# Gate rows turned ahead of the seven-product stage, with two narrow gate blocks and a new block order

## The chip, the core and the metric

The kernel runs on one core of a Trainium2 chip. A core has five engines that run at the same time, each its own instructions in order: TensorE (PE, matrix products), VectorE (DVE), ScalarE (ACT), GpSimd (POOL) and SyncE (SP). They wait for each other through semaphores. DMAs are issued from the queues of SyncE and ScalarE here. The metric is the time of one execution in microseconds; the median of three runs of the kernel before is 2293.48 us (2289.91 to 2294.73).

## The reference, cut to what matters

The reference is one decoder layer in float32 with 512 tokens and a width of 2048. One wide input projection of the normalised input `u` feeds two branches; their outputs are projected back, gated, added and normalised.

```python
u = _rmsnorm(h, norm_w)
proj = jnp.matmul(u, w_in)
(ml_q, ml_k, ml_v, ml_o, ml_z, ml_i, ml_f,
 dn_qkv, dn_z, dn_b, dn_a, gate_a, gate_b) = jnp.split(proj, idx, axis=-1)

i_pre = _softcap(ml_i + ml_i_bias).transpose(0, 2, 1)
logf = jax.nn.log_sigmoid(_softcap(ml_f + ml_f_bias)).transpose(0, 2, 1)
h_a = _mlstm_chunkwise(q, k, v, i_pre, logf)           # 8 heads
h_a = _merge_heads(_rmsnorm(h_a)) * ml_norm_w
h_a = h_a * jax.nn.sigmoid(ml_o) * jax.nn.silu(ml_z)

beta = jax.nn.sigmoid(dn_b).transpose(0, 2, 1)
g = (-jnp.exp(dn_a_log) * jax.nn.softplus(dn_a + dn_dt_bias)).transpose(0, 2, 1)
h_b = _gated_delta_chunkwise(dq, dk, dv, beta, g)      # 16 heads
h_b = _merge_heads(_rmsnorm(h_b, dn_norm_w)) * jax.nn.silu(dn_z)

y = sigmoid(gate_a) * (h_a @ w_out[:2048]) + sigmoid(gate_b) * (h_b @ w_out[2048:])
out = _rmsnorm(x + y, final_norm_w)
```

The four small column groups `ml_i`, `ml_f`, `dn_b` and `dn_a` (48 columns together) are the gate rows of the title: they are summed and scanned along the tokens before either branch can use them.

## The kernel before, in words

Each float32 operand is split into a high part and a remainder (`split_hi` on ScalarE, L128; `split_lo` on VectorE, L131), and each product is made of three products of parts. Weights come by DMA on SyncE's queue into tiles `wr` (four), and their parts stand in tiles `wh` and `wl` (four each). `plan` lists all weight pieces in order of use; `next_w` loads four pieces ahead and splits three ahead.

TensorE's instructions stand in the order in which the code is written. Work of other kinds is put between its products by generators: `start(gen, wait)` enters one, and `tick()`, called once for every few products, resumes those whose waiting time has come; `yield n` waits n ticks. For the other engines a planner sets the order, by its own estimate of times and by priorities (`urgent`, `behind`, `high_priority`); on the chip each engine keeps that order.

The stages are:

1. Front. `u` is made and turned (L304 to L311), and the projection ML_Q runs with it (`proj_cm`, 96 products of 512 columns, L240 to L242, 16 ticks). The 48 gate columns are accumulated beside it in `pgr` (L318), copied to `gr0` (L342) and stored in DRAM as `gr_d` (L343). The projection ML_K follows, and one narrow block of the merge gates (`narrow_gates`, `proj_tm`, 192 products of 256 columns, L255 to L258, 16 ticks). Beside these run `u_sums` (L355 to L370), which makes eight pairs' sums of parts of `u` on GpSimd, VectorE and ScalarE, and `lead` (L550), which loads the first weight quads and prepares the first.
2. Seven-product stage (`seven`, L448). Nine blocks, each of which makes two 512-column projections from seven products of sums in place of eight: three blocks of merge gates (kind g), two of values (v), four of z and output gate (z). A block has 16 quads; a quad has three loads into `wr3`, sums on VectorE (`prep_sums`, L399: `t13` at L410, `ts` at L411 and L417), and splits (`prep_pair`). Sums of products go into the tile `X` (`U1`, `C22`) by `add` (L442). What each block does with its results is in `sink_flat` and `sink_z`, whose output tiles share the four `wr` buffers; they are stored in `tg_d`, `v_d` and `g_d`.
3. `gates` (L589 to L675) loads `gr_d` back, turns it to token columns (`pgt`, L595), computes the gate functions on VectorE and ScalarE in small tiles `sml` (L598 to L627), ten ticks later turns them to rows (`pri`, `prf`, `prg`, L636 to L638), scans the rows (L651 to L654), makes `nr`, `ar`, `er` and `iw`, stores rows in `rows_d`, and six ticks later turns rows to columns again (`pc`, L668 to L670). Two narrow gate blocks run beside this. `ml_first` prepares the first pair of mLSTM heads, from 21 ticks on.
4. Units (`UNITS`): eight pairs of DeltaNet heads (`dn_unit`, four projections each) and the other three pairs of mLSTM heads (`ml_unit`, two). A unit's recurrences run as generators under the projections of the next units; `dn_back` has short chains of TensorE and ScalarE (L880 to L915).
5. The last narrow gate block, with `load_h(0, 1)` beside it, which reloads the branch output `h` from DRAM (L1169 to L1173, ScalarE at L1171); then the output projections (L1214 and L1256 to L1258), the merge and the final norm.

The tiles of the seven-product stage (pools `sbp` and `sap`) are given up at its end, and the pool `wk` of the units takes their memory; its first writes, `gr` and `mkq` (L1128) among them, wait for that.

Of the kernel before, what the change touches and what calls it, by code (L numbers as in the profile page):

```python
# [8 lines left out]
F32 = mybir.dt.float32  # L9
# [17 lines left out]
GFIRST = (1, 3)  # L27
# [29 lines left out]
def hybrid_body(  # L57
# [31 lines left out]
    gr_d = dr.tile([112, S], F32, tag="grd", name="gr_d")  # L89
# [53 lines left out]
    add_gates(range(GFIRST[0]))  # L143
    nfront = len(plan)
    add_gates(range(*GFIRST))
# [3 lines left out]
    add_gates(range(GFIRST[1], GNARROW))  # L149
# [193 lines left out]
    nc.scalar.dma_start(gr_d, gr0)  # L343
# [27 lines left out]

    quads = [(kind, c1, c2, b, g, i) for b, (kind, c1, c2) in enumerate(SEVEN) for g in "AB" for i in range(KH)]
    rawq, partq = [], []

    def load_quad():
        if len(rawq) == len(quads):
            return
        _, c1, c2, b, g, i = quads[len(rawq)]
        with tc.high_priority(offset=2 * PRIO):
            r = sbp.tile([P, 3, NO], F32, tag="wr3", name="wr3", bufs=3)  # L380
            k1, k2 = (slice((2 * i + n) * P, (2 * i + n + 1) * P) for n in range(2))
            if g == "A":
                src = (w_in[k1, c1:c1 + NO], w_in[k1, c2:c2 + NO], w_in[k2, c2:c2 + NO])
            else:
                src = (w_in[k2, c1:c1 + NO], w_in[k2, c2:c2 + NO], t2_d[b % 2, i])
            for n in range(3):
                nc.sync.dma_start(r[:, n, :], src[n])
        rawq.append(r)

    def split(src, wide):  # L390
        if wide:
            hi, lo = (sbp.tile([P, 2, NO], F32R, tag=f"w2{n}", name=f"w{n}", bufs=2) for n in "hl")
        else:
            hi, lo = (wp.tile([P, 1, NO], F32R, tag=f"w{n}", name=f"w{n}", bufs=NSPL) for n in "hl")
        split_hi(hi, src)
        split_lo(lo, src, hi)
        return [(hi[:, n, :], lo[:, n, :]) for n in range(2 if wide else 1)]

    def prep_sums(q):  # L399

        if q >= len(quads) or q < len(partq):
            return
        _, c1, c2, b, g, i = quads[q]
        r = rawq[q]
        with tc.high_priority(offset=2 * PRIO):
            ts = wp.tile([P, 1, NO], F32, tag="tg", name="ts", bufs=3)
            if g == "A":

                t13 = sbp.tile([P, 2, NO], F32, tag="t13", name="t13")
                V.tensor_tensor(out=t13, in0=r[:, 1:3, :], in1=r[:, 0:2, :], op=ALU.subtract)  # L410
                V.tensor_tensor(out=ts[:, 0, :], in0=r[:, 2, :], in1=t13[:, 0, :], op=ALU.subtract)  # L411
                p_ = split(ts, False)
                nc.scalar.dma_start(t2_d[b % 2, i], ts[:, 0, :])
                partq.append((p_ + split(r[:, 0:1, :], False), t13))
            else:

                V.tensor_tensor(out=ts[:, 0, :], in0=r[:, 0, :], in1=r[:, 2, :], op=ALU.subtract)  # L417
                partq.append((split(ts, False), r[:, 0:2, :]))

    def prep_pair(q):  # L420
        if q < len(quads):
            p_, pair = partq[q]
            with tc.high_priority(offset=2 * PRIO):
                w2 = split(pair, True)
            partq[q] = p_ + w2 if quads[q][4] == "A" else w2 + p_

    JW, OO = ((psj, "pj"), (psw, "wk")), ((pso, "o"),) * 2

    def half2(t):
        return slice(HP + t.start, HP + t.stop)  # L430

    LHS = {"A": (lambda i, t: (suh[:, i, 1, t], sul[:, i, 1, t]),
                 lambda i, t: (uh[:, 2 * i, t], ul[:, 2 * i, t]),
                 lambda i, t: (suh[:, i, 0, t], sul[:, i, 0, t]),
                 lambda i, t: (suh[:, i, 2, t], sul[:, i, 2, t])),
           "B": (lambda i, t: (uh[:, 2 * i + 1, t], ul[:, 2 * i + 1, t]),
                 lambda i, t: (s4h[:, i, t], s4l[:, i, t]),
                 lambda i, t: (uh[:, 2 * i + 1, half2(t)], ul[:, 2 * i + 1, half2(t)]))}

    def add(x, a, b):  # L440
        with urgent(3):
            V.tensor_tensor(out=x, in0=a, in1=b, op=ALU.add)  # L442

    def copy1(t, p1):
        with urgent(3):
            A.copy(U1[t], p1)

    def seven(n0, kind, c1, c2):  # L448

        m6, m1, m5, m7 = ([pool.tile([P, NO], F32, tag=t, name="ps") for pool, t in banks_] for banks_ in (OO, JW, JW, JW))  # L450
        ends = {"A": (None, lambda t: (copy1(t, m1[t]), add(U1[t], U1[t], m6[t])),
                      lambda t: add(C22[t], U1[t], m5[t]), lambda t: add(C22[t], C22[t], m7[t])),
                "B": SINK[kind](c1, c2, m1, m5, m7)}
        for n in range(2 * KH):
            g, i = "AB"[n // KH], n % KH
            prep_sums(n0 + n + 1)
            prep_pair(n0 + n + 1)
            load_quad()
            if n == 2 * KH - 2:

                prep_sums(n0 + n + 2)
            if n0 + n == len(quads) - 1:
                limit[0] = len(plan)
                prepare(nfront - 1)
            for m, ps in enumerate((m6, m1, m5, m7) if g == "A" else (m1, m5, m7)):
                hi, lo = partq[n0 + n][m]
                for t in range(2):
                    ah, al = LHS[g][m](i, slice(t * P, (t + 1) * P))
                    T.matmul(ps[t], ah, hi, start=(g == "A" and i == 0), stop=False, skip_group_check=True)  # L469
                    T.matmul(ps[t], ah, lo, start=False, stop=False, skip_group_check=True)  # L470
                    T.matmul(ps[t], al, hi, start=False, stop=(i == KH - 1), skip_group_check=True)  # L471
                    if i == KH - 1 and ends[g][m] is not None:
                        ends[g][m](t)
                tick()

    def stored(q, d, x_):
        with behind("A"):
            nc.scalar.dma_start(d, x_)
        yield 1

    def sink_flat(dst, func, scale):

        def sink(c1, c2, m1, m5, m7):
            def out_(ps, c, col):
                o = wp.tile([P, NO], F32, tag="wr", name="to", bufs=NRAW)
                with urgent(3):
                    A.activation(o, ps, func, scale=scale)  # L487
                nc.scalar.dma_start(dst(c, col), o)

            def late(x_, c, col):  # L490
                with behind("A"):
                    if func != AF.Copy:
                        A.activation(x_, x_, func, scale=scale)
                    nc.scalar.dma_start(dst(c, col), x_)
                yield 1

            def end5(t):
                add(m5[t], U1[t], m5[t])
                out_(m5[t], t, c2)
                start(late(C22[t], 2 + t, c2), 1)  # L500

            def end7(t):
                add(U1[t], U1[t], m7[t])
                start(late(U1[t], 2 + t, c1), 2)

            return (lambda t: out_(m1[t], t, c1)), end5, end7
        return sink

    def sink_z(c1, c2, m1, m5, m7):

        col = c1 - ML_Z
        zs = {}

        def end1(t):
            z = wp.tile([P, NO], F32, tag="wr", name="to", bufs=NRAW)
            with urgent(3):
# [4 lines left out]
        def end5(t):  # L521
            add(m5[t], U1[t], m5[t])
            with urgent(3):
# [4 lines left out]
        def late(t):  # L528
            th = wp.tile([P, NO], F32, tag="wr", name="to", bufs=NRAW)
            with behind("A"):  # L530
                A.activation(th, U1[t], AF.Tanh, scale=0.5)
                A.activation(C22[t], C22[t], AF.Tanh, scale=0.5)
# [790 lines left out]
```

## Time and profile before

| what | value |
|---|---|
| median of three runs | 2293.48 us |
| the profiled execution | 2289.74 us |
| its span, first to last instruction | 2288.0 us |
| mean granted TensorE clock | 0.993 |
| TensorE busy | 2219.1 us (97%) |
| VectorE busy | 1516.8 us (66%) |
| ScalarE busy | 892.2 us (39%) |
| GpSimd busy | 262.0 us (11%) |
| DMA traffic | 384.97 MB, mean 168 GB/s |

In the rows of the profile `L240` is line 240 of the kernel, PE to SP are the engines (`SPq` and `ACTq` their DMA queues), `out<-in` are the program's tiles, and `xN` counts instructions. A row of the timeline gives start and duration in us, and in brackets the idle time of the engine before the instruction and what ended it. A row of the waits gives who waited for whom, the total in us, how often and the longest. A row of the windows gives length, the busy time of each engine with its count of instructions, the granted clock, the share of the DMA engines and GB/s.

### The profile page before, as it was taken

The numbers are of one execution on the slowest core, as the hardware profiler recorded it, in microseconds if no ns is written. First come the engines' busy times: TensorE is split into PE (matmuls) and PEld (weight loads), VectorE is DVE, ScalarE is ACT, GpSimd is POOL, SyncE is SP. The second block draws the span as 40 slices with busy tenths as digits, with TensorE's granted clock in tenths as the row PEclk, the third lists the DMA queues.
The fourth block names the chain that finished last, engine by engine and source line by source line (L and its number), as shares of the span: only waits on it lengthen the run. The fifth ranks groups of instructions, "written<-read, shape, count | busy, mean of one in ns | idle before, by whom it ended". The sixth has DMA issues, their size and how long they took to land.

```text
span 2288.0 us, 33006 instructions
## 1 busy us (share of the span) xinstructions
PE 2219.1 (97%) x11599; PEld 1857.0 (81%) x11599; DVE 1516.8 (66%) x2721; ACT 892.2 (39%) x1768; POOL 262.0 (11%) x329
## 2 busy tenths in 40 slices
PE   6999999999999989999999999999999999999998
PEld 5878887878777878878887888888888889987886
DVE  5878777777887854858367673868458685434445
ACT  4344444444444433433343343343343344222223
POOL 0700000000000001202022110212013210000111
PEclk9999999999999989999999999999999999999999
DMA  5367767776666646557466484656566465865333
GB/s 152 115 200 229 232 182 226 228 221 184 207 210 186 216 135 165 138 128 189 109 157 145 118 208 105 163 135 170 137 146 152 118 161 181 247 209 162 116 116 131
DMA packets 503721, 384.97 MB, mean 168 GB/s; under 512 B 238369, under 2 KB 402434, under 8 KB 503554
## 3 DMA queue, kind: packets, MB, share of 16 engines
q1 hardware_dynamic: 406146, 333.26, 51.9%
q10 hardware_dynamic: 97408, 49.60, 7.4%
q8 instruction: 91, 1.49, 0.3%
q14 instruction: 76, 0.62, 0.1%
HBM read 310.09 MB, written 72.65 MB: 167 GB/s over the span
## 4 chain that ended last, share of the span: by engine, by line
PE 69%; DMA 12%; DVE 10%; issue 3%; ACT 2%; SPq 2%; POOL 1%; ACTq 0%; DVEq 0%; POOLq 0%
PE pj L240 12%; PE pj L241 11%; PE pj L242 11%; PE ps L469 5%; PE ps L470 5%; PE ps L471 5%; DVE wl L131 4%; DMA wr<-t_d 3%; PE py L1257 3%; PE py L1258 3%; PE py L1256 3%; DMA wr<-in_w_in_dram 2%; DMA hr<-h_d 2%; PE pjt L255 1%; PE pjt L258 1%
## 5 line engine op out<-in xcount | busy, mean ns | idle before, releaser
L131 DVE TENSOR_TENSOR wl<-wr,wh 128x512 fp32r<-128x512 f32 (+1 forms) x624 | 490.1, 789 | 354.4 <-ACT wh L128 333.5
L128 ACT CAST wh<-wr 128x512 fp32r<-128x512 f32 (+1 forms) x624 | 415.9, 669 | 722.0 <-PE pj L241 359.3
L240 PE MATMUL pj<-uh,wh 128*128 128x512 f32 x1280 | 530.1, 414 | 3.8 <-ACT thz L721 3.2
L242 PE MATMUL pj<-uh,wl 128*128 128x512 f32 x1280 | 501.3, 392 | 0.0
L241 PE MATMUL pj<-ul,wh 128*128 128x512 f32 x1280 | 500.5, 391 | 0.6 <-DVE ul L310 0.6
L242 PEld LDWEIGHTS pj<-uh,wl 128*128 128x128 f32 x1280 | 240.6, 188 | 52.8
L240 PEld LDWEIGHTS pj<-uh,wh 128*128 128x128 f32 x1280 | 241.6, 189 | 50.4 <-ACT thz L721 3.6
L241 PEld LDWEIGHTS pj<-ul,wh 128*128 128x128 f32 x1280 | 241.8, 189 | 43.9 <-DVE ul L310 0.9
L469 PE MATMUL ps<-wh,suh 128*128 128x512 f32 x432 | 169.6, 393 | 6.1 <-DVE X L442 2.5
L470 PE MATMUL ps<-wl,uh 128*128 128x512 f32 x432 | 169.4, 392 | 1.7 <-DVE wl L131 1.7
L469 PE MATMUL ps<-wh,uh 128*128 128x512 f32 x432 | 169.2, 392 | 1.6 <-DVE X L442 0.9
L470 PE MATMUL ps<-wl,suh 128*128 128x512 f32 x432 | 168.3, 390 | 0.7 <-DVE wl L131 0.7
L471 PE MATMUL ps<-wh,ul 128*128 128x512 f32 x432 | 168.2, 389 | 0.0
L471 PE MATMUL ps<-wh,sul 128*128 128x512 f32 x432 | 168.2, 389 | 0.0
L257 PE MATMUL pjt<-wl,uh 128*128 128x256 f32 x512 | 147.6, 288 | 2.8 <-DVE wl L131 2.8
L255 PE MATMUL pjt<-wh,uh 128*128 128x256 f32 x512 | 149.8, 293 | 0.0
L128 ACT CAST wh<-ts 128x512 fp32r<-128x512 f32 x144 | 89.0, 618 | 151.0 <-DVE ts L417 126.2
L258 PE MATMUL pjt<-wh,ul 128*128 128x256 f32 x512 | 147.3, 288 | 0.0
L128 ACT CAST wh<-t 128x1024 fp32r<-128x1024 f32 x72 | 75.8, 1053 | 181.8 <-DVE ts L411 80.4
L131 DVE TENSOR_TENSOR wl<-t,wh 128x1024 fp32r<-128x1024 f32 x72 | 89.1, 1238 | 47.8 <-ACT wh L128 47.7
L131 DVE TENSOR_TENSOR wl<-ts,wh 128x512 fp32r<-128x512 f32 x144 | 98.6, 690 | 20.8 <-ACT wh L128 20.8
L469 PEld LDWEIGHTS ps<-wh,suh 128*128 128x128 f32 x432 | 81.1, 188 | 28.0 <-ACT to L487 4.5
(284 smaller groups left out, 3705.7 us busy)
## 6 DMA issues: line engine op xcount, KB each, us to landing
wr<-in_w_in_dram SPq DMA_DIRECT2D x712, 256.0 KB, 3.5
wr<-in_w_out_dram SPq DMA_DIRECT2D x128, 256.0 KB, 3.2
t_d<-ts ACTq DMA_DIRECT2D x72, 256.0 KB, 3.6
wr<-t_d SPq DMA_DIRECT2D x72, 256.0 KB, 4.1
tgl<-tg_d SPq DMA_DIRECT2D x24, 256.0 KB, 3.5
xt<-in_x_dram SPq DMA_DIRECT2D x8, 512.0 KB, 7.9
v<-v_d SPq DMA_DIRECT2D x8, 512.0 KB, 5.6
mg<-g_d SPq DMA_DIRECT2D x16, 256.0 KB, 3.3
```

Source lines behind the costliest of these rows:

```text
L128: newest["A"] = A.copy(hi, src).ins
L131: newest["V"] = V.tensor_tensor(out=lo, in0=src, in1=hi.bitcast(F32), op=ALU.subtract).ins
L240: T.matmul(ps[j], hi[:, k, wsl], uh[:, kt, :], start=(kt == 0), stop=False)
L241: T.matmul(ps[j], hi[:, k, wsl], ul[:, kt, :], start=False, stop=False)
L242: T.matmul(ps[j], lo[:, k, wsl], uh[:, kt, :], start=False, stop=(kt == KT - 1))
L255: T.matmul(o, uh[:, kt, tsl], hi[:, k, :], start=(kt == 0 and c % 2 == 0), stop=False, skip_group_check=True)
L257: T.matmul(o, uh[:, kt, tsl], lo[:, k, :], start=False, stop=False, skip_group_check=True)
L258: T.matmul(o, ul[:, kt, tsl], hi[:, k, :], start=False, stop=(kt == KT - 1), skip_group_check=True)
L469: T.matmul(ps[t], ah, hi, start=(g == "A" and i == 0), stop=False, skip_group_check=True)
L470: T.matmul(ps[t], ah, lo, start=False, stop=False, skip_group_check=True)
L471: T.matmul(ps[t], al, hi, start=False, stop=(i == KH - 1), skip_group_check=True)
L1256: T.matmul(ps[c], hh[base][:, kt, tsl], hi[:, 0, :], start=(kt == 0), stop=False)
```

## The change

`gates` moves from behind the seven-product stage to its front: it starts with ML_K, takes `gr0` from its tile, without the store to and load from DRAM, and keeps its rows in the stage's own tiles (`wr3` for rows, `t13` for `sml`) before the first quads need them. Some rows reuse others' places, so `ar` is made before `nr`, and `er` after `iw`. `u_sums` starts 8 ticks later and `lead` at 38 ticks in place of 24. Two narrow gate blocks stand ahead of the stage in place of one, none at the head of the units in place of two, and two behind the units in place of one, with `load_h` beside the second. `ml_first` starts one tick into the first unit.

In the stage the order of the blocks is z, g, v. The sums of a block's first quad are made one quad sooner. `sink_z` only copies the first product out of PSUM and takes one tanh of the second ahead of the next block; the rest follows later. The last block's output tiles come from `tg` in place of `wr`.

```diff
-GFIRST = (1, 3)
+GFIRST = 2
...
-SEVEN = ([("g", GATE + c, GATE + c + NO) for c in range(GNARROW * NB, 2 * D, 2 * NO)]
-         + [("v", ML_V + c, ML_V + c + NO) for c in range(0, 2 * D // 2, 2 * NO)]
-         + [("z", ML_Z + c, ML_O + c) for c in range(0, D, NO)])
+SEVEN = ([("z", ML_Z + c, ML_O + c) for c in range(0, D, NO)]
+         + [("g", GATE + c, GATE + c + NO) for c in range(GNARROW * NB, 2 * D, 2 * NO)]
+         + [("v", ML_V + c, ML_V + c + NO) for c in range(0, D, 2 * NO)])
...
-    nc.scalar.dma_start(gr_d, gr0)
...
     def gates():
-        gr0 = wk.tile([112, S], F32, tag="th", name="gr1", bufs=3)
-        nc.sync.dma_start(gr0, gr_d)
-        yield 5
+        rows = [sbp.tile([P, 3, S], F32, tag="wr3", name="grow", bufs=3) for _ in range(3)]
+
+        def row(n, i):
+            return rows[i // 3][0:n, i % 3, :]
+
...
-        sml = wk.tile([P, 10, NC, 24], F32, tag="ls", name="sml", bufs=1)
+        sml = sbp.tile([P, 2, NO], F32, tag="t13", name="sml").rearrange("p a n -> p (a n)")[:, 0:240 * NC]
...
+        iw, ar, nr, er = row(MLH, 7), ir, br, mr
+        V.tensor_tensor(out=ar, in0=ir, in1=br, op=ALU.subtract)
         V.tensor_tensor(out=nr, in0=br, in1=mr, op=ALU.subtract)
-        V.tensor_tensor(out=ar, in0=ir, in1=br, op=ALU.subtract)
-        A.activation(er, mr, AF.Exp, scale=-1.0)
...
+        A.activation(er, mr, AF.Exp, scale=-1.0)
...
     def seven(n0, kind, c1, c2):
...
-            if n == 2 * KH - 2:
+            if n == 2 * KH - 3:
 
-                prep_sums(n0 + n + 2)
+                prep_sums(n0 + n + 3)
...
+    def spare(last):
+        return wp.tile([P, NO], F32, tag="tg" if last else "wr", name="to", bufs=3 if last else NRAW)
...
     def sink_z(c1, c2, m1, m5, m7, last):
...
         def end1(t):
-            z = wp.tile([P, NO], F32, tag="wr", name="to", bufs=NRAW)
+            zs[t] = spare(False)
             with urgent(3):
-                A.activation(z, m1[t], AF.Tanh, scale=0.5)
-                V.scalar_tensor_tensor(out=z, in0=z, scalar=1.0, in1=m1[t], op0=ALU.add, op1=ALU.mult)
-            zs[t] = z
+                A.copy(zs[t], m1[t])
 
         def end5(t):
             add(m5[t], U1[t], m5[t])
+            os_[t] = spare(False)
             with urgent(3):
-                A.activation(m5[t], m5[t], AF.Tanh, scale=0.5)
-                V.scalar_tensor_tensor(out=zs[t], in0=m5[t], scalar=1.0, in1=zs[t], op0=ALU.add, op1=ALU.mult)
-            start(stored(None, g_d[t, :, col:col + NO], zs[t]), 1)
+                A.activation(os_[t], m5[t], AF.Tanh, scale=0.5)
+            start(late(zs[t], os_[t], t), 2 + 2 * t)
...
-    start(u_sums())
-    start(lead(), 24)
+    start(gates())
+    start(u_sums(), 8)
+    start(lead(), 38)
     spill(proj_cm(ML_K), 2, 1.0)
-    for b in range(GFIRST[0]):
+    for b in range(GFIRST):
         narrow_gates(b)
...
-    start(gates())
-    start(ml_first(*ml_new(0)), 21)
-    for b in range(*GFIRST):
-        narrow_gates(b)
+    start(ml_first(*ml_new(0)), 1)
     for kind, p in UNITS:
         (dn_unit if kind == "d" else ml_unit)(p)
...
-    start(load_h(0, 1), 4)
-    for b in range(GFIRST[1], GNARROW):
+    for b in range(GFIRST, GNARROW):
+        if b == GNARROW - 1:
+            start(load_h(0, 1), 4)
         narrow_gates(b)
```

More of the change, by code (lines that the diff above doesn't have):

```diff
@@ L370, in u_sums @@
             yield 3
[L372 to L458, printed above, removed]
-            if n == 2 * KH - 2:
-                prep_sums(n0 + n + 2)
[L462 to L507, printed above, removed]
@@ L638, in gates @@
             T.transpose(prg[0:DNH, tsl], sp[:, c, 8:24], ident)
[L640 to L643 removed]
+        ir, fr, gr, msk = row(MLH, 0), row(MLH, 1), row(DNH, 2), row(DNH, 3)
         A.copy(ir, pri[0:MLH, :])
```

225 lines of the change are left out of this document (164 added, 61 removed).

## The prediction

> **What bounds the kernel now.** I read the page first, then the windows by stage, TensorE's waits, and the timelines of the three places that the change touches. From the page:
>
> ```profile
> PE 2219.1 (97%) x11599; PEld 1857.0 (81%) x11599; DVE 1516.8 (66%) x2721; ACT 892.2 (39%) x1768; POOL 262.0 (11%) x329
> PEclk9999999999999989999999999999999999999999
> PE 69%; DMA 12%; DVE 10%; issue 3%; ACT 2%; SPq 2%; POOL 1%; ACTq 0%; DVEq 0%; POOLq 0%
> ```
>
> TensorE is busy 97% of the span, and the change removes none of its products. So only stretches in which TensorE waits, or runs at a lower granted clock, can move the time. These windows enclose the places (us, PE busy, PEld, DVE, ACT, POOL, granted clock, DMA share, GB/s):
>
> ```profile
> 58.60:80.30 21.70, 21.70 (x97) 17.77 (x96) 17.59 (x15) 10.41 (x18) 16.93 (x14) 1.00 0.69 217
> 80.30:108.30 28.00, 25.23 (x194) 24.73 (x193) 23.61 (x21) 9.62 (x17) 21.47 (x19) 0.94 0.20 58
> 108.30:119.00 10.70, 7.29 (x31) 5.11 (x30) 9.21 (x10) 3.57 (x8) 6.63 (x5) 1.00 0.46 148
> 818.00:837.00 19.00, 8.48 (x71) 8.31 (x71) 7.70 (x13) 4.14 (x8) 2.74 (x14) 0.79 0.67 207
> 837.00:843.00 6.00, 6.00 (x30) 6.00 (x31) 3.83 (x15) 0.80 (x3) 0.00 (x0) 0.51 0.63 216
> 843.00:877.00 34.00, 34.00 (x291) 33.59 (x290) 18.29 (x40) 10.28 (x20) 1.65 (x4) 1.00 0.55 159
> 1893.00:1909.00 16.00, 13.32 (x150) 12.58 (x150) 8.04 (x13) 9.65 (x17) 0.00 (x0) 0.89 0.60 185
> ```
>
> The first row, the second projection (ML_K), has no wait: 96 products in 21.7 us, 0.226 us each. A product of a narrow gate block is half as wide; 843:877 gives 34.0 / 291 = 0.117 with two dozen transposes among them, and I use 0.12, so 192 of them are 23.0 us. TensorE's waits, by who ended them:
>
> ```profile
> PE pgt L595 <- DMA mkq<-qk_d: 10.5, 1, 10.5
> PE ps L469 <- DVE X L442: 4.8, 12, 0.9
> PE pjt L257 <- DVE wl L131: 2.8, 2, 2.2
> PE ps L470 <- DVE wl L131: 2.4, 3, 1.5
> PE p L895 <- ACT s L889: 1.5, 2, 1.3
> PE p L906 <- DVE ta L902: 1.2, 1, 1.2
> ```
>
> **The change, part by part.** The sum is made against the profiled execution, 2289.74 us, of which 2288.0 is the span; the median of the runs, 2293.48, stands 3.7 above it, and I add that at the end.
>
> (a) The 10.5 us wait goes. It lies between the seven-product stage and the units: the gate rows came back from DRAM only after SyncE's queue had issued seven weight loads, and those began late, since the last blocks (kind z) held their tiles until stored.
>
> ```profile
> 823.51 7.80 SPq L165 DMA_DIRECT2D wr<-in_w_in_dram  x7
> 831.48 0.34 SPq L591 DMA_DIRECT2D gr<-gr_d  x1
> 831.87 1.84 SPq L1128 DMA_DIRECT2D mkq<-qk_d  x4
> ```
>
> With it goes a stretch at half clock: in 837:843, at 0.51, 30 products and transposes went in 6.0 us where 6.0 / 0.12 = 50 would have gone, 20 x 0.12 = 2.4 us. Together -12.9. What is late next there: the changed program's order on SyncE has the four mkq loads, which wait for the stage's memory, behind weight loads for eight sub-steps of the first unit, 8 x 12 x 0.226 = 21.7 us of cover; the first product that reads mkq stands 13 ticks of six products in, 13 x 1.36 = 17.7 us, while before the loads began some 14 us after the stage. The first unit now shares VectorE and ScalarE with head pair 0, which had two narrow blocks to itself; I take +1, between 0 and the 5 us that a lost row broadcast would cost (12 us late less the cover above).
>
> (b) The narrow block in front and the start of the stage. 80.30:108.30 took 28.0 for 23.0 us of products: 5.0 lost. 108.30:119 ran 31 products, 31 x 0.226 = 7.0 of 10.7 us: 3.7 lost. Both are VectorE arrears (wl L131 above): it makes the sums of u, weight splits and the first quad's sums together, busy 23.61 of 28 us. After the change a second narrow block, 23 us, stands there, u_sums starts 8 ticks later and lead at 38 of 48 ticks, so the arrears are worked off before the stage. Of 8.7 I take 7.2 back (bounds 0 and 8.7).
>
> (c) The tail. In 1893:1909 PE is busy 13.32 of 16 us, 2.7 idle, at clock 0.89, (1 - 0.89) x 16 = 1.7: 4.4 lost. ScalarE stood at the reloads of h (L1171) while the last unit's L889 and L900 waited behind it:
>
> ```profile
> 1895.53 0.72 ACT L1171 ACTIVATE uh<-hr,normc 128x512 fp32r<-128x512 f32 x1 [1.03 <-DMA hr<-hm_d]
> 1896.78 0.78 ACT L889 ACTIVATE s<-p 32x256 f32<-32x256 f32 x2
> ```
>
> Now a narrow block of 16 ticks is between, and load_h begins in the second one: -4.4 (bounds -4.4 and 0).
>
> (d) Block edges. The ps waits on X at L442 are 4.8 us over 12 times. Earlier first sums, and z sinks that take only a copy or one tanh ahead of the next block, may take 2 of that; two more ScalarE copies per z block, 8 x 0.6 us, are hidden (ACT 39%). -2, bounds -4.8 and +3.
>
> (e) The new cost: the row transposes. All of the gate arithmetic, one block in the old trace, moves into ML_K, among u_sums and the splits. VectorE runs in order, and TensorE reaches the transposes of pri, prf, prg after 11 ticks. Rows of the old trace for what stands ahead of them, and for the chain itself:
>
> ```profile
> 58.63 0.40 PE L240 MATMUL pj<-uh,wh 128*128 128x512 f32 x1
> 60.27 0.73 POOL L362 TENSOR_TENSOR X<-X 128x256 f32<-128x256 f32 x1 [42.33 <-DVE X L359]
> 72.47 1.21 DVE L359 TENSOR_TENSOR X<-uh,ul 128x1024 f32<-128x1024 f32 x1
> 74.47 0.41 DVE L369 TENSOR_TENSOR s4l<-X,s4h 128x256 fp32r<-128x256 f32 x1
> 78.68 3.21 POOL L359 TENSOR_TENSOR X<-uh,ul 128x1024 f32<-128x1024 f32 x1
> 78.68 0.96 DVE L369 TENSOR_TENSOR sul<-X,suh 128x768 fp32r<-128x768 f32 x1 [1.50 <-ACT suh L368]
> 79.56 2.62 DVE L369 TENSOR_TENSOR s4l<-X,s4h 128x256 fp32r<-128x256 f32 x1
> 82.73 1.18 POOL L364 TENSOR_TENSOR X<-X 128x256 f32<-128x256 f32 x1
> 837.92 0.36 DVE L598 COPY gt<-pgt 128x192 f32<-128x192 f32 x1 [7.00 <-DMA mkq<-qk_d]
> 843.70 0.69 DVE L131 TENSOR_TENSOR wl<-wr,wh 128x512 fp32r<-128x512 f32 x1 [1.25 <-ACT wh L128]
> 848.54 0.26 DVE L622 TENSOR_TENSOR sml<-sml 128x96 f32<-128x96 f32 x1
> 850.19 0.22 DVE L627 SCALAR_TENSOR_TENSOR sml<-sml 128x64 f32<-128x64 f32 x1
> ```
>
> ML_K begins at 58.63, so TensorE is there at 58.63 + 66 x 0.226 + four transposes (0.8) = 74.4. In the changed program's order on VectorE the last links of the gate chain stand behind the sul and s4l of the third K pair. GpSimd paces those; nothing of the change makes it faster, and in the old trace that s4l ended at 82.18. Behind it come L620, L621, L622, L623, L624 and L627, about 1.5 us by their starts: 83.7 at the earliest. The chain alone is 8 us (12.5 from its first row to its last, less three splits like the one shown, 0.6 each, and 2.4 of waits), on top of the 17.59 busy us of 58.6:80.3, less some later splits, so I take 84.8. The wait is 10.4 us, as long as the one removed, and I give it the same half-clock price: +12.8 (bounds 9.3 without a clock loss, and 19).
>
> (f) The second row wait. After 12 transposes, 30 products and half a gate sub-step TensorE wants pc. By then VectorE must copy two rows, scan three, make ar and nr with two sul, an X and two splits between; ScalarE then has ML_K's two spills, a split, four exps and er.
>
> ```profile
> 857.01 1.20 DVE L653 TENSOR_TENSOR_SCAN br<-msk,fr 8x512 f32<-8x512 f32 x1
> 861.88 0.97 ACT L661 ACTIVATE iw<-nr,mr 8x128 f32<-8x128 f32 x3
> 859.36 0.63 ACT L658 ACTIVATE er<-mr 8x512 f32<-8x512 f32 x1 [3.14 <-DVE mr L654]
> ```
>
> VectorE: 3 x 1.13 for the scans, 4 x 0.62 for copies and differences, 0.9 + 1.2 + 0.4 for the u ops, 2 x 0.62 to 1.2 for splits: some 10 to 11 us from the rows' arrival; then iw and er, 0.3 + 0.97 + 0.63. That is 12 to 13 us against 1.0 (copies overlap transposes) + 30 x 0.226 + 1.5 = 8.3 to 9. Wait 4, and 1.7 for half clock: +5.7 (bounds 1 and 9). If ScalarE's late spills were all, it would be 1.
>
> By the rule of the Trainium skill, page TensorE: Matmul & The Clock Gate, section Part 1: The HAM clock gate, an idle window of about 3.4 us halves the clock until a busy window has passed; the clock part of (e) would then be 1.7 to 3.4, an estimate from that page, where I took 2.4 from 837:843; the 0.51 of that row agrees with a half.
>
> Removed DMAs (one store, one load of gate rows) and moved transposes cost nothing net. Sum: -12.9 + 1 - 7.2 - 4.4 - 2 + 12.8 + 5.7 = -7.0. Profiled 2282.7, median 2286.4; I say 2286.
>
> **The rivals.**
> R1, the row transposes are covered: the chain's order lets TensorE through with under 5 us in (e) and (f). For it: 18.5 us of front wait is more than any place of the old trace shows. Against: s4l of pair three ended at 82.18. Time 2286 - 13 = 2273.
>
> R2, slower: VectorE and GpSimd take turns on the gate chain. s4l takes 0.41 us alone and 2.62 beside GpSimd's add, ending when that does (82.18 against 81.89). If each of the chain's 12 two-input ops waits out half of a 0.73 to 1.2 us GpSimd op, 12 x 0.5 = 6 more at (e), 3 at (f), and the arrears reach the stage, so that (b) gives nothing, 7: 2286 + 16 = 2302. It decides from 7 us of extra lateness on. Against: ops of 0.2 us fit between GpSimd's. The Trainium skill, page SBUF — State Buffer, section Who interferes with whom, has it that a VectorE instruction with two SBUF inputs blocks fully while a GpSimd instruction that reads SBUF holds their shared port; the s4l row agrees, and R2 is what that rule would make of the chain.
>
> R3, no change: the wait is only moved, 12.9 gone in the middle and 18.5 come in front, with (b), (c) and (d) giving about 6: 2293. That the middle wait stays, as a wait of the first unit on mkq, is the form in which the change would not do what it says; the 17.7 us of cover speak against it.
>
> **How the numbers follow.** Within 0.2% (4.6 us) a measurement cannot tell a change here. Forecast 0.45, of which 0.35 ends below 2288.9 and 0.10 within; its own range is 2279 to 2293. R1 0.20, faster. R2 0.20, slower. R3 0.15: 0.12 within, 0.03 faster. Faster 0.58, same 0.22, slower 0.20. The range runs from below R1, with (d) at its better bound, 2269, to R2, 2302.
>
> **What would show it.** Right: no wait over 2 us between the last ps product and the first unit, granted clock 1.00 there; a wait of 8 to 13 us at the prf transposes ended by VectorE, one of 2 to 6 at pc ended by ScalarE's er, both followed by a 0.5 clock; the narrow blocks after them and the first quads without wl waits; L889 and L900 of the last unit without waits. Wrong: front waits under 5 us in all (R1), narrow blocks and quads still waiting for wl (R2), or new waits over 5 us in the first two units.

## The result, and the profile after

The changed kernel takes 2298.76 us, the kernel before 2291.4 us (medians of 13 runs each): a ratio of 1.0037, with an interval of 1.0027 to 1.0047. It is slower by 0.4%, some 8 us, where 2286 was predicted. The profiled execution took 2297.73 us. From its page:

```profile
PE 2220.8 (97%) x11599; PEld 1856.4 (81%) x11599; DVE 1514.0 (66%) x2721; ACT 896.3 (39%) x1776; POOL 262.0 (11%) x329
PEclk9799999999999999999999999999999999999999
```

Busy times stand as before. The dip of the clock in the second slice is new. The windows of the stages tell where the time went; first the kernel before: ML_K up to the seven-product stage (the front), that stage, the middle, the units, the tail up to the first output projection, and the rest (columns as in the prediction):

```profile
58.60:108.40 49.80, 47.03 (x290) 42.61 (x288) 41.30 (x35) 20.13 (x35) 38.50 (x32) 0.97 0.41 127
108.40:817.40 709.00, 697.36 (x3026) 563.86 (x3025) 552.98 (x690) 311.65 (x444) 6.53 (x5) 1.00 0.66 205
817.40:879.70 62.30, 51.78 (x414) 51.16 (x413) 31.12 (x70) 17.71 (x37) 4.58 (x19) 0.89 0.61 178
879.70:1878.90 999.20, 990.76 (x5390) 824.33 (x5389) 680.63 (x1603) 388.97 (x978) 182.16 (x236) 1.00 0.60 146
1878.90:2011.00 132.10, 129.06 (x1143) 127.85 (x1142) 60.10 (x97) 44.55 (x91) 5.89 (x8) 0.99 0.69 207
2011.00:2288.00 277.00, 263.05 (x1154) 215.56 (x1152) 120.69 (x175) 80.41 (x144) 21.03 (x16) 0.99 0.45 145
```

The same of the changed kernel, where the middle is only 0.2 us:

```profile
59.00:153.30 94.30, 76.08 (x509) 70.50 (x508) 69.71 (x91) 31.85 (x59) 43.57 (x38) 0.87 0.35 102
153.30:864.00 710.70, 698.99 (x3026) 563.59 (x3025) 546.82 (x691) 314.90 (x449) 0.00 (x0) 1.00 0.65 203
864.20:1866.90 1002.70, 992.31 (x5388) 825.19 (x5387) 681.73 (x1607) 390.34 (x982) 188.57 (x253) 1.00 0.61 151
1866.90:2021.60 154.70, 150.92 (x1334) 149.43 (x1333) 66.65 (x108) 52.14 (x105) 5.53 (x8) 1.00 0.66 198
2021.60:2295.90 274.30, 262.28 (x1154) 215.89 (x1152) 118.94 (x172) 78.47 (x140) 21.03 (x16) 0.99 0.44 143
```

A narrow block is 23.0 us. Two left the middle, one went to the front and one to the tail. Less these, the front grew by 94.3 - 49.8 - 23.0 = 21.5 us, the middle fell by 62.3 - 46.0 - 0.2 = 16.1, the tail by 0.4 and the rest by 2.7; the stage grew by 1.7 and the units by 3.5. With 0.4 us by which ML_K begins later that is +7.9, the difference of the spans. So the middle gave what it was to give; the front took more, and the stage, the units and the tail gave nothing. Among TensorE's waits in the changed kernel (left out is the longest, 15.1 us for a load at the start, which was 15.0 before):

```profile
PE prf L426 <- DVE sml L413: 12.6, 1, 12.6
PE pcs L1053 <- DVE kw L1042: 6.8, 5, 3.9
PE pc L455 <- ACT grow L446: 5.6, 1, 5.6
PE ps L559 <- DVE X L532: 4.5, 10, 1.6
PE ps L560 <- DVE wl L130: 3.5, 6, 0.8
PE pr L931 <- DVE st L952: 1.5, 1, 1.5
PE pst L946 <- ACT w L942: 1.4, 1, 1.4
```

The waits at pgt, at L889's and at L902's results (the kernel before's lines) are gone. In their place stand the two row waits of the front, one at pcs in the first unit and two in the last DeltaNet chain. Behind the first three of them the clock is a half (windows of the changed kernel):

```profile
87.40:91.50 4.10, 4.10 (x16) 2.91 (x17) 1.84 (x4) 1.61 (x3) 0.00 (x0) 0.50 0.00 0
104.80:112.00 7.20, 7.20 (x38) 7.17 (x39) 5.08 (x9) 1.87 (x4) 4.92 (x7) 0.50 0.65 172
901.20:907.30 6.10, 6.10 (x14) 4.83 (x15) 2.94 (x5) 4.46 (x14) 2.58 (x4) 0.50 0.84 200
```

At half speed, half of each stretch is lost: 2.1, 3.6 and 3.1 us. The first wait ends with the gate chain on VectorE. Rows of that chain, of a split among it and of GpSimd beside it, from the timeline of the changed kernel:

```profile
61.77 0.42 DVE L394 TENSOR_TENSOR sml<-grow,bia 128x64 f32<-128x64 f32 x1
63.70 2.72 POOL L356 TENSOR_TENSOR X<-uh,ul 128x1024 f32<-128x1024 f32 x1
64.09 2.37 DVE L398 TENSOR_SCALAR sml<-sml 128x32 f32<-128x32 f32 x1
79.06 2.34 POOL L356 TENSOR_TENSOR X<-uh,ul 128x1024 f32<-128x1024 f32 x1
79.08 2.43 DVE L409 TENSOR_TENSOR sml<-sml 128x96 f32<-128x96 f32 x1
83.43 0.42 DVE L366 TENSOR_TENSOR s4l<-X,s4h 128x256 fp32r<-128x256 f32 x1
87.19 0.22 DVE L416 SCALAR_TENSOR_TENSOR sml<-sml 128x64 f32<-128x64 f32 x1
```

L394 to L416 takes 25.6 us. The two steps shown, of 32 and of 96 elements, start just after a wide add of GpSimd and end when it ends (66.46 and 66.42 us, 81.51 and 81.40): VectorE and GpSimd take turns.

### The profile page after: what moved, and what is told of

Read it like the earlier page. It is cut to its first block, busy times and chain, and to the rows that moved or that the text cites. A ratio compares the mean times of both kernels' runs of the same rounds, so it can differ in the third digit from the quotient of the medians.

```text
span 2295.9 us, 32990 instructions
## 1 busy us (share of the span) xinstructions
PE 2220.8 (97%) x11599; PEld 1856.4 (81%) x11599; DVE 1514.0 (66%) x2721; ACT 896.3 (39%) x1776; POOL 262.0 (11%) x329
## 4 chain that ended last, share of the span: by engine, by line
PE 73%; DVE 10%; DMA 9%; issue 3%; ACT 2%; SPq 2%; POOL 0%; ACTq 0%; DVEq 0%; POOLq 0%
PE pj L238 11%; PE pj L239 11%; PE pj L240 11%; PE ps L560 6%; PE ps L559 6%; PE ps L561 5%; DVE wl L130 4%; PE py L1249 3%; PE py L1250 3%; PE py L1248 3%; DMA wr<-in_w_in_dram 2%; PE pjt L253 2%; PE pjt L255 2%; PE pjt L256 2%; DMA wr<-t_d 2%
## 5 line engine op out<-in xcount | busy, mean ns | idle before, releaser
L500 DVE TENSOR_TENSOR t<-wr 128x1024 f32<-128x1024 f32 x72 | 87.8, 1219 | 20.9 <-DMA wr<-in_w_in_dram 20.5
```

## The experiments

T1: the loss is made in front, because the gate chain shares VectorE with the sums of u and takes turns with GpSimd, and its results come later than the products between can cover. The rivals: VectorE's arrears have a fixed size and only surface there; or the loss lies in the stage (sums, z sinks) or at the first unit. Names and lines in the diffs are those of the changed kernel; all ratios are to the kernel before, with the changed kernel at 1.0037.

**More products between.**

```diff
-        yield 10
+        yield 20
...
-        yield 6
+        yield 10
```

> T1 (the gate chain reaches TensorE late because it shares VectorE with the sums of u and their splits, and the changed kernel gives it too few products of cover: 11 ticks before the transposes of prf, some 30 products before pc): with 10 more ticks of ten half-width products and 4 more before pc, the waits at prf (12.6 us) and pc (5.6) and the half clock behind them (2.2 and 3.7) go, to under 4 us in all, and nothing else moves: 18 to 20 us faster than the changed kernel, about 2279, so also faster than the kernel before by some 12. Rival A (the arrears of VectorE only show there and are paid further on): the prf and pc waits go, but waits of ps or of the gate product for wl of 8 to 15 us in all come in the second narrow block and the first quads, and the time falls by 5 us or less. Rival B (the products in between need work of VectorE that stands behind the chain): the waits stay above 10 us.

2292.68 us, 1.0007 (0.9994 to 1.0019): some 6 us faster, a third of what T1 gave. The wait at prf is gone, the front 84.3 us in place of 94.3. But pc still waits 4.4 us, and at 86.2 the first narrow block waits 3.9 us for its bank, which ML_K's spill (L333) has to empty. ScalarE:

```profile
88.79 0.83 ACT L365 CAST suh<-X 128x768 fp32r<-128x768 f32 x1 [5.88 <-POOL X L360]
89.53 0.59 ACT L333 ACTIVATE qk<-pj 128x512 f32<-128x512 f32 x1
```

The spill stands behind a split of the sums of u, which waits 5.9 us for GpSimd. The gate chain is no shorter; its last step begins 28.7 us after ML_K does, 28.2 in the changed kernel. So cover alone isn't enough: it hides the chain without making it shorter, and the spill's wait takes its place.

**The sums of u behind the gate chain.** The first wide add waits for the chain's last VectorE step.

```diff
-            E.tensor_tensor(out=uf, in0=uh[:, 2 * i:2 * i + 2, :].bitcast(F32), in1=ul[:, 2 * i:2 * i + 2, :].bitcast(F32),
-                            op=ALU.add)
+            with ExitStack() as after_:
+                if i == 0:
+                    after_.enter_context(behind("gate"))
+                E.tensor_tensor(out=uf, in0=uh[:, 2 * i:2 * i + 2, :].bitcast(F32),
+                                in1=ul[:, 2 * i:2 * i + 2, :].bitcast(F32), op=ALU.add)
...
-        V.scalar_tensor_tensor(out=sp[:, :, 8:24], in0=sp[:, :, 8:24], scalar=-1.0,
-                               in1=ea.unsqueeze(1).to_broadcast([P, NC, 16]), op0=ALU.mult, op1=ALU.mult)
+        newest["gate"] = V.scalar_tensor_tensor(out=sp[:, :, 8:24], in0=sp[:, :, 8:24], scalar=-1.0,
+                               in1=ea.unsqueeze(1).to_broadcast([P, NC, 16]), op0=ALU.mult, op1=ALU.mult).ins
```

> The first add of the sums of u is held until the last VectorE step of the gate chain has been issued, so the chain runs without those sums and without GpSimd beside it. T1: the wait at prf falls from 12.6 to between 0 and 4 us, that at pc from 5.6 to between 2 and 6 (the sums of u then stand between the scans); the stage's first quads start with sums that end some 12 us later, cover 20 us, so few of them wait: 10 to 14 us faster than the changed kernel, about 2287. Rival A (arrears are only moved): prf falls, and the same 10 to 13 us come back as wl or sul waits at the start of the seven-product stage. Rival C (the chain is slow by its own length and the splits of ML_K): prf stays above 9 us.

2287.40 us, 0.9986 (0.9975 to 0.9997): 11 us faster than the changed kernel, as T1 had it. No wait at prf is left. The chain's seven repeats of two steps, first in the changed kernel:

```profile
L409 DVE TENSOR_TENSOR sml<-sml x7: 249/258/2432, 71.8 to 83.8; 128x96 f32<-128x96 f32 x7
L410 DVE TENSOR_SCALAR sml<-sml x7: 195/210/723, 72.1 to 84.6; 128x96 f32<-128x96 f32 x7
```

and here (shortest, median and longest in ns, first and last start in us):

```profile
L412 DVE TENSOR_TENSOR sml<-sml x7: 251/259/259, 68.8 to 73.7; 128x96 f32<-128x96 f32 x7
L413 DVE TENSOR_SCALAR sml<-sml x7: 201/209/211, 69.1 to 74.0; 128x96 f32<-128x96 f32 x7
```

All of the chain's VectorE steps on `sml` sum to 7.1 us here and to 16.9 in the changed kernel: 9.8 us of the chain are turns with GpSimd. From its first row to its last it takes 11.5 us in place of 25.6; the other 4.3 us are the sums and splits that no longer stand between. The wait at pc is 6.7 us in two pieces, just above the 2 to 6 expected, with a half clock behind it.

**No wide add on GpSimd.**

```diff
-            E = V if i % 2 == 0 else G
+            E = V
```

> All four wide adds of the sums of u go on VectorE (1.2 us each) and none on GpSimd (3 us each). If turns with GpSimd stretch the gate chain (rival R2 of the prediction, in its mechanism): the two-input steps of the chain that took 0.7 to 2.4 us beside GpSimd go to 0.3 us, the wait at prf falls by 3 to 6 us and the time by 4 to 8. If VectorE's own load sets it: VectorE has 2.4 us more to do ahead of the transposes, and the wait at prf is 0 to 3 us longer, the time the same or up to 4 us longer.

2291.79 us, 0.9997 (0.9986 to 1.0009): 7 us faster, the wait at prf 9.9 us in place of 12.6 and the one at pc 3.4 in place of 5.6. VectorE has four adds more in the front and yet is busy 63.9 us there, not 69.7. So its load isn't the bound; the turns are. The rest of the chain is still stretched by GpSimd's 256-element steps (L409's median here is 0.67 us).

**er ahead of iw.**

```diff
-        iw, ar, nr, er = row(MLH, 7), ir, br, mr
+        iw, ar, nr, er = row(MLH, 7), ir, br, fr
...
+        A.activation(er, mr, AF.Exp, scale=-1.0)
         A.activation(iw[:, 0:P], nr[:, 0:P], AF.Exp)
...
-        A.activation(er, mr, AF.Exp, scale=-1.0)
```

> The row er is computed ahead of the three exps of iw instead of behind them, in a row of its own. If the wait at pc (5.6 us, ended by ScalarE's er) is set by ScalarE's order: it falls by 1.0 to 1.5 us and the time by 1 to 2 us, within what can be told. If it is set by the scans on VectorE alone, er starts no earlier and the wait is 5 to 6 us. No theory expects more than 2.5 us here; the wait at prf stays at 12 to 13.

2295.22 us, 1.0017 (1.0006 to 1.0027), 3.5 us faster: more than any theory allowed. The wait at pc is gone; 1.6 us for the spill stand in its place. ScalarE in the changed kernel, then here:

```profile
100.09 0.83 ACT L365 CAST suh<-X 128x768 fp32r<-128x768 f32 x1 [4.84 <-POOL X L360]
104.10 0.63 ACT L446 ACTIVATE grow<-grow 8x512 f32<-8x512 f32 x1
```

```profile
95.63 0.63 ACT L443 ACTIVATE grow<-grow 8x512 f32<-8x512 f32 x1 [2.68 <-DVE grow L438]
100.50 0.83 ACT L365 CAST suh<-X 128x768 fp32r<-128x768 f32 x1 [3.73 <-POOL X L360]
```

er is made from the row mr alone, whose scan (L439) ended at 92.1 in the changed kernel. But there er is written over mr, so it has to stand behind nr and the exps of iw, which still read mr, and with them behind a split of the sums of u that waited 4.84 us for GpSimd. The edit writes er over fr instead; it starts when the last scan that reads fr (L438) has ended, 8.5 us sooner.

**The first sums of a block one quad later, as before the change.**

```diff
-            if n == 2 * KH - 3:
+            if n == 2 * KH - 2:
...
-                prep_sums(n0 + n + 3)
+                prep_sums(n0 + n + 2)
```

> The changed kernel with the first sums of a block's first quad made when they were before. If making them one quad sooner is what puts VectorE behind at the block's second half (the waits on X at the ninth quad, up to 1.75 us, in 5 of 9 blocks): these shrink and the stage falls from 710.7 to 707 or 708 us. If making them sooner helps at the edges, as the prediction had it: waits at the first quad come back, 0.7 to 1.3 us a block, and the stage takes 713 to 718. If neither: 709 to 712, and no difference in time beyond 2 us.

2296.59 us, 1.0033 (1.0021 to 1.0044); by time alone it can't be told from the changed kernel. The stage can:

```profile
154.70:861.70 707.00, 696.85 (x3026) 563.94 (x3025) 548.72 (x691) 315.60 (x449) 0.00 (x0) 1.00 0.66 205
```

707.0 in place of 710.7, and this holds in every kernel here: the seven with the changed z handling and early sums take 709.7 to 712.0 us, the five with late sums 705.8 to 708.5. So the early sums cost 3 to 4 us. The waits on X stay, though (4.8 us in 9, in place of 4.5 in 10), those at the ninth quad among them (up to 1.2 us): that they are the way by which it costs is not shown.

**The old handling of the z blocks.** `sink_z` and `late` as they were: both tanh and their products ahead of the next block, the first store at once.

```diff
-                A.copy(zs[t], m1[t])
+                A.activation(z, m1[t], AF.Tanh, scale=0.5)
+                V.scalar_tensor_tensor(out=z, in0=z, scalar=1.0, in1=m1[t], op0=ALU.add, op1=ALU.mult)
...
-            start(late(zs[t], os_[t], t), 2 + 2 * t)
+            start(stored(None, g_d[t, :, col:col + NO], zs[t]), 1)
```

> The changed kernel with the old handling of the z blocks' results (both tanh and the products taken ahead of the next block). The prediction put a gain of some 2 us on the new handling. If it gives one: the waits of 0.8 to 1.0 us at the third quad (four blocks) move back to the first, and the stage is 1 to 4 us longer, 712 to 715. If the new handling only moves the wait: the stage stays at 709 to 712 and the time within 2 us of the changed kernel. If it costs: the stage falls by 2 or more. The front stays as it is, at 89 to 94 us.

2300.93 us, 1.0049 (1.0033 to 1.0066), the stage 713.6 us, and the waits on X 9.6 us in 15 in place of 4.5 in 10. By time it can't be told from the changed kernel either; the stage is 1.6 us above the longest of the seven. As expected, the waits at the third quad of the four blocks behind a z block move back to the first, and grow from 0.4 to 0.8 us to 1.2 to 1.3. So the new handling gives some 3 us, as the prediction had it; the early sums take them back.

**One narrow block back at the head of the units, one behind them.**

```diff
-GFIRST = 2
+GFIRST, GHEAD = 2, 1
...
     start(ml_first(*ml_new(0)), 1)
+    for b in range(GFIRST, GFIRST + GHEAD):
+        narrow_gates(b)
```

> The changed kernel with one narrow block back between the stage and the units, so head pair 0 has 23 us of products without another unit beside it; one narrow block is left behind the units, with the reload of h in it, as before the change. If head pair 0 in the first unit costs what the units lost (3.9 us at pcs and half a clock from 900.5 to 907.3, 3.4): both go, and the way from the stage's end to the last projection is 5 to 7 us shorter. If two narrow blocks behind the units are what took away L889's and L900's waits at the last unit: those come back, 4.4 us, and the sum is 0 to 3 us faster. If neither: within 2 us of the changed kernel. The front stays.

2300.48 us, 1.0047 (1.0029 to 1.0065): no gain. Units, tail, and the two waits in question:

```profile
887.40:1885.40 998.00, 990.29 (x5380) 824.27 (x5380) 683.04 (x1603) 390.71 (x980) 184.62 (x239) 1.00 0.60 148
1885.40:2018.60 133.20, 130.34 (x1142) 129.01 (x1141) 59.85 (x97) 44.53 (x91) 5.90 (x8) 0.97 0.69 206
```

```profile
PE pcs L1054 <- DVE kw L1043: 5.8, 3, 4.5
PE p L890 <- ACT s L884: 2.0, 1, 2.0
```

The wait at pcs stays at 4.5 us: a narrow block for head pair 0 ahead of the first unit doesn't take it away. Less that block, the way from the stage's end to the tail is 3.7 us shorter (1002.9 to 999.2), but the tail is 1.5 and the rest 3.8 longer. With one block behind the units ScalarE's wait comes back (2.0 us) with a half clock of 6.8 us: the tail is 133.2 - 23.0 = 110.2 us in place of 108.7. The mechanism of step (c) is there; in the tail it is worth 1.5 us.

**pc later, behind the sums edit.** As the second experiment, and

```diff
-        yield 6
+        yield 12
```

> As the kernel whose sums of u wait for the gate chain (2287.4 us, span 2285.8), and pc six ticks later. There the waits at pc were 2.1 and 4.6 us, 6.7 in all, and half a clock followed from 90.6 to 97.4, 3.4 us lost. T1 (only cover is lacking, the row work itself is short): six more ticks are 8.6 us of products, so pc does not wait, nor does the clock fall there: 9 to 10 us less, about 2278, the front from ML_K to the stage 73 to 75 us in place of 83.5. Rival A (the arrears are moved on): the pc wait goes, but the narrow blocks wait for ScalarE's tgs (2.2 us already) and the first quads for sul or wl, 5 us or more in all: about 2283 or above.

2285.71 us, 0.9977 (0.9965 to 0.9989), the front 78.7 us. pc no longer waits, but 5.9 us of other waits come instead, as the rival had it: the narrow blocks wait 3.1 and 0.9 us, the second quad 1.9. VectorE:

```profile
108.34 1.76 DVE L503 TENSOR_TENSOR t<-wr 128x1024 f32<-128x1024 f32 x1 [1.30 <-DMA wr<-in_w_in_dram]
110.03 1.22 DVE L130 TENSOR_TENSOR wl<-wr,wh 128x512 fp32r<-128x512 f32 x1
```

The rows stand in the tiles of the first quads until pc is done, so these loads come late, and the narrow block's weight split is queued behind the sum that waits for them.

**All that helped, and two more edits.** The ninth kernel has the second experiment's edit, er first, late sums, and `yield 8`. The tenth adds to it the first line below, the eleventh the second, the twelfth both.

```diff
-    start(ml_first(*ml_new(0)), 1)
+    start(ml_first(*ml_new(0)), 5)
...
-            E = V if i % 2 == 0 else G
+            E = V
```

> The sums of u wait for the gate chain; er is computed ahead of the exps of iw; pc comes 2 ticks later (8, where 12 put the return of the rows' tiles, and so the first quads' loads, too late: 1.3 us of VectorE waiting for a load with the weight splits behind it); the first quad's sums are made when they were before the change. T1: no wait at prf, none or under 1 us at pc, no wl wait over 1 us in the narrow blocks, one half clock of 3.4 us at most in the front: front 73 to 77 us (78.7 with pc at 12 ticks, 94.3 in the changed kernel), stage 707 to 709, about 2279 to 2281. Rival (VectorE's arrears in front have a fixed size, 8 us or so, whatever the order): the front stays at 78 to 81 us and the time at 2283 to 2286.

> The same with the first mLSTM head pair started 4 ticks later in the first unit. If the wait at pcs (4 to 5 us, with half a clock for 3.4 to 6.8 us behind it) comes from the pair's rows and keys, that arrive over DRAM at a fixed time after the stage: 4 ticks are 5.4 us of products, the wait goes, and the units take 997 to 999 us in place of 1001 to 1003: 3 to 5 us faster than the same kernel without it. If the wait is VectorE's work of the first unit and the pair's own, in turn: it moves by 4 ticks and stays, within 1.5 us.

> As the first of these, with all four wide adds of the sums of u on VectorE, none on GpSimd. With the chain out of the way the adds stand beside splits only. If GpSimd's long adds hold VectorE up still (s4l 2.6 us beside them, 0.4 alone): the sums end earlier, ScalarE's tgs no longer waits behind suh, the front is 2 to 4 us shorter. If VectorE is the bound there: 0 to 2 us longer.

> The two last edits together: head pair 0 four ticks later, and no long add of the sums of u on GpSimd. If they are independent (one works at the first unit, one in the front): front 75 us, units 995, so some 4 us below the kernel with the later head pair alone, 2274 to 2275, a ratio to the kernel before of 0.992 to 0.993. If both only gave the same arrears another place: no better than the better of the two, 2278.

| kernel | median, us | ratio (interval) | front, us | stage | units |
|---|---|---|---|---|---|
| ninth | 2281.09 | 0.9952 (0.9933 to 0.9970) | 79.7 | 708.4 | 1002.6 |
| tenth | 2278.22 | 0.9939 (0.9923 to 0.9955) | 78.7 | 708.5 | 995.4 |
| eleventh | 2279.75 | 0.9947 (0.9929 to 0.9965) | 75.1 | 707.6 | 1001.0 |
| twelfth | 2277.09 | 0.9946 (0.9928 to 0.9964) | 75.1 | 705.8 | 998.7 |

All four beat both kernels; among themselves they can't be told apart by time. In the ninth the time came as said, but the front did not: 79.7, inside the rival's range, with 4.5 us of wl waits and 2.0 for tgs. The eleventh shows what about half of these arrears are. Front of the ninth and of the eleventh:

```profile
60.60:140.40 79.80, 73.26 (x510) 68.04 (x510) 66.57 (x91) 31.64 (x59) 48.66 (x38) 0.98 0.39 111
```

```profile
58.90:134.00 75.10, 72.87 (x509) 67.92 (x508) 62.93 (x95) 31.34 (x59) 35.60 (x34) 0.98 0.41 118
```

With four adds more VectorE is busy 3.6 us less and TensorE done 4.6 us sooner (3.6 us in the twelfth against the tenth): the arrears have no fixed size. The ninth's front is 8.8 us longer than its products (21.7, 46.0 and 3.2 us); some 4 of these are turns with GpSimd. ScalarE's tgs, against what was expected, still holds TensorE up for 1.9 us. In the tenth the first wait at pcs falls from 4.0 to 0.8 us, and no half clock follows:

```profile
890.43 0.67 PE L1056 MATMUL pcs<-v,kw 128*128 128x257 f32 x2 [0.79 <-DVE kw L1045]
```

In the changed kernel and in the seventh, kw was scaled 36 and 38 us after the stage's end, without a narrow block between and with one. What it stood behind in the changed kernel:

```profile
899.40 0.69 DVE L130 TENSOR_TENSOR wl<-wr,wh 128x512 fp32r<-128x512 f32 x1 [0.91 <-ACT wh L127]
900.01 1.12 DVE L1042 TENSOR_TENSOR kw<-kw,we 128x512 f32<-128x512 f32 x1
```

kw goes to DRAM and back, but its load, issued at 887.36, had landed by 894.2 (no transfer of kw took over 6.8 us). VectorE came to it some 6 us later, behind a split of a weight of the first unit (`wl`). The first half of that split, `wh` on ScalarE, began at 898.75, after 2.47 us of waiting for the weight's load. The seventh, ninth and eleventh kernels have the same order; in the tenth and the twelfth the split ahead waits for no load. So what comes last is a weight load, not kw; why these loads are late, no run here takes apart. Whether the last two edits add up stays open: the twelfth's profiled execution is the shortest (span 2268.1 us), but its median can't be told from those of the tenth and the eleventh.

## Why the prediction was wrong

The sign was wrong. No single step explains it: the terms came out worse by 15 us together (+7.9 for -7.0). The two waits in front stood where the prediction put them, and every sign that it named for being right came; so did one of those for being wrong, new waits of over 5 us in the first two units (5.3 at pcs). The bounds held but for (d) and (f), by 1.0 and 0.2 us; the values chosen between them did not.

| step | predicted | measured | how |
|---|---|---|---|
| (a) the middle | -12.9 | -12.9 | -16.1, of which 3.2 is 27 transposes that moved in front, 0.117 us each as in 843:877 |
| (a) first unit | +1 | +3.5 | units 999.2 to 1002.7 |
| (b) narrow block in front | -5.0 | -5.6 | what is left of the front's +21.5 less 3.2, 14.7 and 9.2 |
| (b) start of the stage | -2.2 | -2.3 | its first block, 81.6 to 79.3 us |
| (c) tail | -4.4 | -0.4 | tail 132.1 to 154.7, less 23.0 |
| (d) block edges | -2 | +4.0 | stage +1.7, less the first block |
| (e) wait at prf | +12.8 | +14.7 | 12.6 and 2.1 of clock |
| (f) wait at pc | +5.7 | +9.2 | 5.6 and 3.6 of clock |
| ML_K's start | 0 | +0.4 | |
| output projections and after | 0 | -2.7 | 277.0 to 274.3 us |

(d) failed most, by 6 us, and in sign. "Earlier first sums ... may take 2 of that": they cost 3 to 4 (fifth experiment). What the z sinks gave (3 us, sixth) is lost on them. Some 3 to 4 us more lie in the three blocks of kind g, which take 236.2 us before, the arrears at the stage's start included, 237.0 in the changed kernel and 237.3 in the fifth experiment; the four z blocks take 315.5, 315.4 and 312.9, the two v blocks 157.7, 158.8 and 157.2. Why isn't known: the block order wasn't tried by itself. The first block is of kind g before and z after, so the line between (b) and (d) is a rough one: by the waits in it before, 3.4 us, (b) would be -3.4 there and (d) +5.1.

(c) failed by 4 us. L889 and L900 no longer hold TensorE up, as forecast, which is the 2.7 us of waits and 1.7 of clock. But the step took what is gained there as gained in all, and the last DeltaNet chain waits behind them instead: 3.8 us at pr, pst and po, where 0.4 were before. The 2.7 us at the end are no term of the prediction: the output projections wait 0.7 us for their weights' splits in place of 2.5. The fourth kernel, whose code is the same from there on, waits 4.1 and takes 279.3 us for that part, so this gain isn't firm.

(f) was mis-sized by 3.5 us, 1.6 of wait and 1.9 of clock (7.2 us at half, where 3.4 were reckoned). VectorE's part came as reckoned, 10.9 us from the rows' arrival to the end of nr. ScalarE then needed 4.1 us to the end of er, not 1.9: the prediction listed the work ahead of er but priced it by busy time, and one split among it had waited for GpSimd, with two spills and two more splits behind it (fourth experiment). "If ScalarE's late spills were all, it would be 1" looked at the right queue; what held it was the split ahead of them. The terms on TensorE's side also add up to 9.3 us, not to 8.3 to 9.

(e) was mis-sized by 1.9 us. The last links do stand behind s4l of the third pair, which ended at 83.9 (82.2 in the old trace). But the chain was priced by rows of the old trace beside which GpSimd stood nearly still, where by the same trace it is busy 16.9 of 21.7 us in the new place: the links left, to the end of L416, took 3.6 us, not 1.5. R2 named the mechanism, and its 6 us were too few for the chain itself, 9.8 (second experiment); only 2.2 of them were new at the wait, since the prediction had the chain's end held up by s4l of the third pair already. R2's other half, that the arrears reach the stage, is refuted: the narrow blocks ran without a wait for wl, and the first block was shorter. R2's time, 2302, came closest, but by luck in part: 10 of the 15 us are (d)'s and (c)'s, which R2 didn't have.

(a) was right in the middle. In the first unit the prediction followed the mkq loads, which made it, and not the weight loads behind them in VectorE's order, which end the wait at pcs; the tenth experiment takes most of that wait away with 4 ticks. (b) was right.

## What to carry to other kernels

Price a chain of small VectorE steps at the place it moves to: look at what GpSimd does there, and count a step that starts beside a long GpSimd add as ending with it. When such a chain feeds TensorE through a queue that is served in order, ask for each instruction ahead of it what that one waits for, not how long it runs; here one exp, given a row of its own and moved ahead of a split that waited, took a wait of 5.6 us away, for 1.6 in another place. A move that only exchanges one wait for another can still be worth having once the work beside the moved part is put behind it: with the sums of u held back this change is 0.1% faster than before instead of 0.4% slower, and 0.5% with the smaller edits, one of which takes the early sums back.

## What the runs showed of the hardware

The clock halves for stretches of 3.41 us on a fixed grid (6.83, 10.24 and 13.65 us occur too, two to four of them), and a half-empty stretch can be enough. The twelfth kernel (1.9 us of wait in the first row), and the ninth, with about the same wait twice:

```profile
109.39:112.80 3.41, 1.51 (x13) 1.48 (x13) 2.95 (x4) 2.88 (x6) 1.20 (x2) 1.00 0.54 153
112.80:116.21 3.41, 3.41 (x18) 3.41 (x18) 3.41 (x4) 0.83 (x1) 3.33 (x4) 0.50 0.48 129
```

```profile
111.23:114.64 3.41, 1.72 (x15) 1.52 (x13) 1.92 (x2) 1.95 (x4) 3.25 (x4) 1.00 0.56 151
114.64:118.05 3.41, 3.08 (x25) 3.09 (x26) 3.41 (x3) 1.28 (x3) 2.45 (x3) 1.00 0.01 3
124.89:128.30 3.41, 1.46 (x12) 1.25 (x11) 3.41 (x3) 0.35 (x1) 3.33 (x4) 0.99 0.00 0
128.30:131.71 3.41, 3.41 (x18) 3.41 (x17) 3.07 (x3) 1.92 (x4) 3.33 (x2) 0.51 0.00 0
```

I cut the traces of all fourteen kernels on this grid (each one's own, set by its first half-clock stretch after 20 us), from 25 to 2250 us of the span. Of the stretches at full clock in which TensorE was busy less than 0.455 of the time, 35 of 35 were followed by a half; between 0.455 and 0.565 it was 5 of 20; between 0.565 and 0.9, 1 of 337; above, none. The limits were chosen to part these counts. So in these two kernels a wait of 1.9 us cost 1.7 us more, half a stretch, where it lay within one stretch, and one of 2.0 us nothing more where it spanned two. The Trainium skill, page TensorE: Matmul & The Clock Gate, section Part 1: The HAM clock gate, has a free-running window of 3.4 us, which agrees, and half clock after at least one idle window; here a window 0.44 busy sufficed, and the measurement decides.

L398 has one input of 32 elements and took 2.37 us beside GpSimd's add, 0.17 us without it; the reciprocal L404 took 0.75 us in both. The Trainium skill, page SBUF — State Buffer, section Who interferes with whom, counts tensor_scalar among the operations that can take the shared port pair; the trace agrees.
